# A two-layer hybrid trunk on one core: wider opening products, an earlier filter chain, and a new order of the first opening

## The chip, the cores and the metric

The kernel runs on one core of one Trainium2 chip. The metric is the device time in microseconds (us) of one execution, as the median of several runs. All weights are read from HBM in each run, all arithmetic is float32 or a sum of products whose operands were split into two halves of lower precision.

## The reference, cut to what matters

The input x is 256 rows of 1024 channels. Two layers follow, each a feed-forward block, a mixer of two branches, and a second feed-forward block:

```python
for l in range(DEPTH):                                   # 2
    x = x + 0.5 * swiglu(rms_norm(x), gate, up, down)    # ffn1, d_ff = 2688
    h = rms_norm(x)
    x = x + hybrid_mixer(h, ...)
    x = x + 0.5 * swiglu(rms_norm(x), gate, up, down)    # ffn2

def swiglu(h, w_gate, w_up, w_down):
    return (silu(h @ w_gate) * (h @ w_up)) @ w_down

def hyena_filters(L, w1, b1, w2, b2, w3):                # once a layer, needs no x
    hid = sin(z @ w1 + b1)                               # z: 256 x 33, w1: 33 x 64
    hid = sin(hid @ w2 + b2)                             # w2: 64 x 64
    k = (hid @ w3) * decay                               # w3: 64 x 2048
    full = two_sided(k) * rsqrt(sum(full * full) + EPS)  # unit norm per channel
    return rfft(full)                                    # the spectra of two filters
```

The mixer projects h, runs a Hyena branch (short convolution, two long convolutions by the spectra above) and an attention branch with 12 heads (q and k normed, scores, exp, values), gates the two and projects back.

## The kernel before

All weights pass through one stream of 380 tiles of 128 x 1024 in the order of the list `srcs`: in each layer 65 for ffn1 (among them two for the filters, `fw3`), 62 for the mixer, 63 for ffn2. A tile is loaded into `raw` (four buffers, queue of SP). ACT copies it to `whi` in the short format (line 151), DVE subtracts to get the rest `wlo` (line 58, the line of the helper that records all vector work), both with seven buffers. The activations have the same two halves, `hT[..., 0, :]` (xh) and `hT[..., 1, :]` (xl). A product is three matmuls: wh·xh, wh·xl and wl·xh. One tile feeds 24 matmuls of 256 columns, or 12 of 512.

The stages of an ffn: the **opening** (`opening`, four tiles) makes the first 256 gate and 256 up columns with the tokens as the stationary side, first for token block j = 0 with all four tiles, then for j = 1, since j = 1 is normed later. `xstat` writes the matmuls of one tile and one j. Before the change a tile holds four k-slices of 256 columns of the gate (tiles 0 and 1) or the up weights (tiles 2 and 3). Then 19 pairs of tiles make the remaining columns with the weights stationary, and 21 tiles of the down projection follow. In the very first opening the input has to be squared, normed and transposed first; `warm` products of a zero tile (WARM = 12) run on TensorE before that. `features` transposes the normed x (`xn`) into a PSUM bank, ACT writes the high half of hT and, at a later call, DVE the low half.

Engines run what their queue holds in program order, and the program text is made by a planner. `slot` writes one tile's matmuls, then `passed(UNIT)` takes 2.43 us off `owed`, the vector work that was written and is counted as not yet done (each counted vector instruction adds to it). Before each slot `tick(room)` lets the side chains (`side`) write their next steps while `owed` is under `room` (1.5 us in an ffn, 0.9 to 2.5 in the mixer); a chain that has asked for a wait gets a due time from `owed`, at most 4.86 us. In an opening no slot of j = 0 takes anything off, so `owed` is high when it ends.

Beside ffn1 the side chain `filters` runs: loads into `fc`; a product on 33 rows (`s<-fc`); a sine (eight vector instructions on `sd`, then Sin on ACT, which needs a table load, as does the next Tanh); a product on 64 rows; a second sine; `st`, the third factor; `fw3_unit`, a tile of the main stream; four products with the decay; their squares and sums (`sq`); transposes and a reduction; `rb`, a broadcast on ACT, and its transposes; the scaled `sd`; their halves `hl`; products with the transform matrix `dft`; and the spectra `spec`. All of this twice, once per filter; FW3 = (10, 20) are the pairs m behind which the two `fw3` tiles stand. In the mixer `hyena` and `attention` are the side chains; step n of `attention` writes turn(n - 1), values(n - 2) and scores(n): scores are four products, a reduction on DVE and exp on ACT, `turn` transposes them and copies back, `values` multiplies by v. After the last gate tile the chains are written to their end without other tiles between.

Of the kernel before, what the change touches and what calls it, by code (L numbers as in the profile page):

```python
# [47 lines left out]
def hybrid_trunk(ctx: ExitStack, tc: tile.TileContext, a: dict, out: bass.AP):  # L48
# [88 lines left out]
    def loads(depth=NRAW):  # L137
        while ptr["dma"] < min(len(srcs), ptr["lo"] + depth):
# [3 lines left out]
            nc.sync.dma_start(raws[v][:, :n], src)  # L142
            ptr["dma"] += 1

    def pump_hi():
# [5 lines left out]
        act(out=pairs[v][0][:, :n], in_=raws[v][:, :n], func=AF.Copy)  # L151
# [135 lines left out]
    def normalize(j, mid=None):  # L287
# [4 lines left out]
        if mid is not None:  # L292
            mid()
# [44 lines left out]
    def xstat(acc, i, n, js=(0, 1), c0=0, late=False):  # L338
        kk = DM // n

        def fn(wh, wl):
            for j in js:
                terms = ((0, wh), (1, wh), (0, wl)) if late else ((0, wh), (0, wl), (1, wh))
                for t, (x_, w_) in enumerate(terms):
                    for k in range(kk):
                        g = i * kk + k
                        mm(acc[j][:, c0:c0 + n], hT[:, g, j, x_, :], w_[:, k * n:(k + 1) * n],
                           t == 0 and g == 0, t == 2 and g == KD - 1)
        return fn

    def opening(acc, evac, n):

        us = [use() for _ in range(4)]
        per = n // P

        def part(i, j):
            g, k = divmod(i, per)
            return xstat({j: acc[j][g]}, k, n, (j,), g * n if acc[j][0] is acc[j][-1] else 0, j == 0 and i > 1)

        for i in range(4):  # L360
# [3 lines left out]
            if i in FEAT1:  # L364
                features(1, i - FEAT1[0])()
            for _ in range(FILL[i]):
# [79 lines left out]
    def ffn(l, w, gain, chains=()):  # L446
        with tc.tile_pool(name=nm("ffn"), bufs=1, reuse_waits="tile") as fp:
# [44 lines left out]
            acc = [[bank("acc")] * 2 for _ in range(2)]  # L492

            def first(j):
                t, g, u = t2[:, j, :], acc[j][0][:, :256], acc[j][1][:, 256:]
# [16 lines left out]
            opening(acc, first, 256)  # L512
# [34 lines left out]
    def filters(l):  # L547
        def gen(fp):
            fc = fp.tile([P, S + 2 * P + 2], F32, name=nm("fc"))
            nc.sync.dma_start(fc[:33, :S], a["zT"])  # L550
            nc.sync.dma_start(fc[:33, S:S + P], a["fw1"][l])
            nc.sync.dma_start(fc[:64, S + P:S + 2 * P], a["fw2"][l])
# [30 lines left out]
            mm(b[:, :S], fc[:33, S:S + P], fc[:33, :S], True, True)  # L583
# [3 lines left out]
            mm(b[:, :S], fc[:64, S + P:S + 2 * P], h1[:64, :], True, True)  # L587
# [8 lines left out]
            for o in range(2):  # L596
# [128 lines left out]
    def mixer(l, gain):  # L725
        with tc.tile_pool(name=nm("mix"), bufs=1, reuse_waits="tile") as mp:
# [265 lines left out]
            for blk in range(5):  # L992
# [3 lines left out]
                if blk == 0:  # L996
                    opening([[b] for b in acc], qkv_out(blk, n, acc), n)
# [71 lines left out]
    with tc.manual_schedule():  # L1069
        nc.vector.memset(mhalf, -0.5)  # L1070
        act(out=junk, in_=mhalf[:, :1], func=AF.Tanh)
        warm = spec[:, 0, 0, :P]
# [8 lines left out]
        b = bank("x")  # L1081
        for _ in range(WARM):
            mm(b[:, :P], warm, warm, True, True)
        for h in range(2):
# [147 lines left out]
```

## Time and profile before

| | |
|---|---|
| median of 3 runs | 1120.11 us (1118.97 to 1120.43) |
| profiled execution | 1119.33 us, its span 1117.5 us |
| granted clock, mean | 0.999 |
| TensorE busy | 1102.4 us, 99% |
| VectorE busy | 840.2 us, 75% |
| ScalarE busy | 643.3 us, 58% |
| read from HBM | 204 MB, 184 GB/s |

The times inside the trace count from the start of the span. The profiled execution's own time is 1.8 us longer than its span. A busy TensorE is one that has a matmul in flight; matmuls overlap, so the pace is read from the starts of neighbouring rows. In the list of waits a row gives the engine and the tile that it writes, and after the arrow the engine and the tile that it waited for.

### The profile page before, as it was taken

The page shows a single profiled execution, that of the slowest core. Times are in us where ns is not written, and L with a number is a line of the kernel's source. Part 1 is how long each engine was busy: PE and PEld are TensorE (multiplying, and loading weights), DVE is VectorE, ACT ScalarE, POOL GpSimd, SP SyncE. Part 2 cuts the span into 40 slices and gives each one's busy share as a digit, 9 for nine tenths or more (in the row PEclk, how much of TensorE's full clock was granted, in tenths as well). Part 3 has the DMA queues.
Part 4 walks back from the last instruction along what each step waited for, and adds up shares of the span by engine and source line. Part 5 has one row for each costly group of instructions (what it writes and reads, how often), then busy time and mean ns, then how long its engine had stood idle before and what let it go on. Part 6 is the DMA issues. An engine that isn't in the chain of part 4 may idle for free.

```text
span 1117.5 us, 19195 instructions
## 1 busy us (share of the span) xinstructions
PE 1102.4 (99%) x7591; PEld 1029.3 (92%) x7591; DVE 840.2 (75%) x1243; ACT 643.3 (58%) x983; POOL 64.4 (6%) x113
## 2 busy tenths in 40 slices
PE   9999999999999999999999999999999999999998
PEld 8999988998999999998899998889989998999997
DVE  6779896788865877777567789868888667777772
ACT  6566754665655556666456665547565554666651
POOL 5100000011200000000000000001012000000000
PEclk9999999999999999999999999999999999999999
DMA  8756666556433746667746665737465245666671
GB/s 302 234 168 210 201 212 184 170 171 189 150 115 108 234 140 201 195 193 235 252 147 201 192 209 174 244 110 240 156 185 156 86 125 205 200 192 193 189 256 64
DMA packets 58845, 206.35 MB, mean 185 GB/s; under 512 B 7058, under 2 KB 7718, under 8 KB 58756
## 3 DMA queue, kind: packets, MB, share of 16 engines
q1 hardware_dynamic: 57764, 203.10, 57.3%
q0 software_dynamic: 704, 1.97, 0.6%
q8 instruction: 59, 0.97, 0.4%
q14 instruction: 30, 0.25, 0.1%
q10 hardware_dynamic: 288, 0.07, 0.0%
HBM read 204.00 MB, written 1.11 MB: 184 GB/s over the span
## 4 chain that ended last, share of the span: by engine, by line
PE 82%; DVE 8%; DMA 5%; ACT 3%; issue 2%; POOL 0%; SPq 0%; ACTq 0%; DVEq 0%; POOLq 0%
PE acc L89 54%; PE x L89 13%; PE s L89 12%; DMA raw<-in_gu 4%; DVE wlo L58 3%; PE x L102 2%; DVE spec L58 1%; ACT whi L151 1%; DVE t L58 1%; DVE xn L58 1%; ACT sq L285 1%; DVE x L58 1%; DVE hT L58 1%; PE x L750 1%; PE s L102 0%
## 5 line engine op out<-in xcount | busy, mean ns | idle before, releaser
L58 DVE TENSOR_TENSOR wlo<-raw,whi 128x1024 fp32r<-128x1024 f32 (+1 forms) x380 | 457.6, 1210 | 54.8 <-ACT whi L151 54.5
L151 ACT ACTIVATE whi<-raw 128x1024 fp32r<-128x1024 f32 (+1 forms) x380 | 392.8, 1046 | 142.3 <-PE acc L89 52.6
L89 PE MATMUL acc<-hT,whi 128*128 128x256 f32 (+1 forms) x2416 | 463.5, 290 | 0.0
L89 PEld LDWEIGHTS acc<-hT,whi 128*128 128x128 f32 x2416 | 379.6, 192 | 8.2 <-issue 1.3
L89 PE MATMUL acc<-hT,wlo 128*128 128x256 f32 x1360 | 367.1, 275 | 0.0
L89 PEld LDWEIGHTS acc<-hT,wlo 128*128 128x128 f32 x1360 | 260.9, 192 | 1.9
L89 PE MATMUL acc<-whi,hid 128*128 128x512 f32 (+1 forms) x378 | 115.5, 357 | 0.0
L89 PE MATMUL acc<-whi,hT 128*128 128x256 f32 (+1 forms) x576 | 115.2, 328 | 0.0
L89 PE MATMUL x<-whi,hid 128*128 128x512 f32 x336 | 112.1, 380 | 0.0
L89 PE MATMUL s<-hT,whi 128*128 128x512 f32 x304 | 104.0, 383 | 0.0
L89 PEld LDWEIGHTS acc<-whi,hT 128*128 128x128 f32 x576 | 88.0, 191 | 8.6 <-ACT hT L317 1.1
L89 PEld LDWEIGHTS acc<-whi,hid 128*128 128x128 f32 x378 | 71.0, 189 | 8.6
L89 PE MATMUL s<-hT,wlo 128*128 128x256 f32 x304 | 76.7, 273 | 0.0
L89 PEld LDWEIGHTS x<-whi,hid 128*128 128x128 f32 x336 | 63.6, 189 | 7.9
L89 PE MATMUL acc<-wlo,hid 128*128 128x512 f32 (+1 forms) x189 | 66.4, 356 | 0.0
L89 PEld LDWEIGHTS s<-hT,whi 128*128 128x128 f32 x304 | 57.7, 190 | 6.9 <-DVE c L58 0.7
L89 PE MATMUL acc<-wlo,hT 128*128 128x256 f32 (+1 forms) x288 | 63.4, 324 | 0.4 <-DVE wlo L58 0.2
L89 PE MATMUL x<-wlo,hid 128*128 128x512 f32 x168 | 63.7, 379 | 0.0
L481 ACT ACTIVATE hid<-t 128x256 fp32r<-128x256 f32 x38 | 19.9, 523 | 70.1 <-DVE t L58 70.1
L89 PEld LDWEIGHTS s<-hT,wlo 128*128 128x128 f32 x304 | 58.1, 191 | 1.9
L58 DVE TENSOR_TENSOR hid<-t,hid 128x256 fp32r<-128x256 f32 x76 | 35.5, 466 | 22.4 <-ACT hid L481 22.4
L58 DVE SCALAR_TENSOR_TENSOR t<-t,acc 128x256 f32<-128x256 f32 x46 | 19.2, 417 | 43.0 <-ACT t L457 33.1
(189 smaller groups left out, 1297.4 us busy)
## 6 DMA issues: line engine op xcount, KB each, us to landing
raw<-in_gu SPq DMA_DIRECT2D x152, 512.0 KB, 4.3
raw<-in_dn SPq DMA_DIRECT2D x84, 512.0 KB, 4.4
raw<-in_win_q SPq DMA_DIRECT2D x32, 512.0 KB, 4.0
raw<-in_wg SPq DMA_DIRECT2D x32, 512.0 KB, 4.2
raw<-in_win_h SPq DMA_DIRECT2D x24, 512.0 KB, 4.5
raw<-in_gx SPq DMA_DIRECT2D x16, 512.0 KB, 5.0
raw<-in_wo SPq DMA_DIRECT2D x16, 512.0 KB, 4.1
raw<-in_wp SPq DMA_DIRECT2D x16, 384.0 KB, 3.0
```

Of the source, the lines that this page charges most:

```text
L58: return f(**kw)
L89: nc.tensor.matmul(o, l, r, start=start, stop=stop)
L102: nc.tensor.transpose(b[:, q * P:(q + 1) * P], ap, ident)
L151: act(out=pairs[v][0][:, :n], in_=raws[v][:, :n], func=AF.Copy)
L285: act(out=sq, in_=x[:, j, sl], func=AF.Square, scale=1.0 / 32.0, accum_out=nst[j][:, h:h + 1])
L481: act(out=hi, in_=tv, func=AF.Copy)
L750: nc.tensor.transpose(tb[j][:, (q0 + i) * P:(q0 + i + 1) * P], c[:, i, 1 + j:1 + S:2], ident)
```

## The change

The change has five parts.

The ffn openings use 512-column products: the host lays a tile out as two k-slices of 256 gate and 256 up columns, gate and up of one j share one PSUM bank, and 48 products of 512 columns take the place of 96 of 256. For j = 0 the low halves of the weights now come last in every tile (wh·xh, wh·xl, wl·xh); before, that held for tiles 2 and 3 alone. The mixer's openings, which had 512 columns, get that order too.

In the first opening, `idle` puts a zero product ahead of each term of the first three tiles, nine in all; WARM goes from 12 to 15; tile 0 is loaded in two halves and cast by DVE in two instructions in place of ACT; the calls of the low halves (`los`) and of the pumps stand in another order.

The filter products use all 128 rows: the host pads z, w1 and w2 with zeros, and `fc` is loaded in full (256 KB in place of 83).

At an opening's end `owed` is cut to at most OPEN = 2.0. The filter weights stand sooner: FW3 = (8, 20).

An addition of the skip weights is done for the first of two spectral parts alone (i == 0).

```diff
-WARM = 12
+WARM = 15
+OPEN = 2.0
-FW3 = (10, 20)
+FW3 = (8, 20)
...
-            nc.sync.dma_start(raws[v][:, :n], src)
+            for h in range(2 if v == 0 else 1):
+                sl = slice(h * 512, (h + 1) * 512) if v == 0 else slice(0, n)
+                nc.sync.dma_start(raws[v][:, sl], src[:, sl])
...
-        act(out=pairs[v][0][:, :n], in_=raws[v][:, :n], func=AF.Copy)
+        if by_vector:
+            for h in range(2):
+                sl = slice(h * 512, (h + 1) * 512)
+                dve.tensor_copy(out=pairs[v][0][:, sl], in_=raws[v][:, sl])
+        else:
+            act(out=pairs[v][0][:, :n], in_=raws[v][:, :n], func=AF.Copy)
...
                 for t, (x_, w_) in enumerate(terms):
+                    for _ in range(idle["n"]):
+                        mm(idle["b"], idle["w"], idle["w"], True, True)
...
-            return xstat({j: acc[j][g]}, k, n, (j,), g * n if acc[j][0] is acc[j][-1] else 0, j == 0 and i > 1)
+            return xstat(acc, i, 512, (j,), late=j == 0)
...
+        owed[0] = min(owed[0], OPEN)
...
-            nc.sync.dma_start(fc[:33, :S], a["zT"])
-            nc.sync.dma_start(fc[:33, S:S + P], a["fw1"][l])
-            nc.sync.dma_start(fc[:64, S + P:S + 2 * P], a["fw2"][l])
+            nc.sync.dma_start(fc[:, :S], a["zT"])
+            nc.sync.dma_start(fc[:, S:S + P], a["fw1"][l])
+            nc.sync.dma_start(fc[:, S + P:S + 2 * P], a["fw2"][l])
...
-            mm(b[:, :S], fc[:33, S:S + P], fc[:33, :S], True, True)
+            mm(b[:, :S], fc[:, S:S + P], fc[:, :S], True, True)
...
-            mm(b[:, :S], fc[:64, S + P:S + 2 * P], h1[:64, :], True, True)
+            mm(b[:, :S], fc[:, S + P:S + 2 * P], h1, True, True)
...
-                        if j == 0:
+                        if j == 0 and i == 0:
                             TT(out=t[0:1, :], in0=t[0:1, :], in1=sk[:, o, :], op=ALU.add)
...
-        normalize(0, pump_hi)
+        normalize(0)
+        pump_hi(by_vector=True)
         los = [features(0, 0)]
-        pump(1)
+        pump_hi()
+        los[0]()
+        pump_lo()
         los.append(features(0, 1))
-        los[0]()
-        pump(1)
+        pump_hi()
+        pump_lo()
+        los[1]()
         for h in range(2):
             squares(1, h)
-        los[1]()
         pump_lo()
```

What the change does to the order of instructions is shown at three places. First VectorE in the first opening. A row is one instruction (or several alike), what it writes, and behind the arrow what it reads. Before:

```order
L58 TENSOR_SCALAR v_118<-ss_113 128x1
L58 TENSOR_SCALAR xn_125<-x,r_120 128x512 x2
L58 TENSOR_TENSOR wlo_123<-raw_91,whi_122 128x1024
L58 SCALAR_TENSOR_TENSOR hT<-x_128,gT,hT 128x128 x4
L58 TENSOR_TENSOR wlo_138<-raw_93,whi_137 128x1024
L58 SCALAR_TENSOR_TENSOR hT<-x_143,gT,hT 128x128 x4
L58 TENSOR_TENSOR wlo_157<-raw_95,whi_156 128x1024
L58 TENSOR_SCALAR v_174<-ss_162 128x1
```

And after:

```order
L59 TENSOR_SCALAR v_122<-ss_117 128x1
L59 TENSOR_SCALAR xn_126<-x,r_124 128x512 x2
L157 CAST whi_129<-raw_91 128x512 x2
L59 SCALAR_TENSOR_TENSOR hT<-x_133,gT,hT 128x128 x4
L59 TENSOR_TENSOR wlo_130<-raw_91,whi_129 128x1024
L59 TENSOR_TENSOR wlo_143<-raw_94,whi_142 128x1024
L59 SCALAR_TENSOR_TENSOR hT<-x_152,gT,hT 128x128 x4
L59 TENSOR_TENSOR wlo_162<-raw_96,whi_161 128x1024
L59 TENSOR_SCALAR v_179<-ss_171 128x1
```

The two casts of tile 0 are new, the first low half of the features moved ahead of the first `wlo`, and the second behind that of tile 1.

Second VectorE around `st` in ffn1 of layer 0. `t` and `hid` belong to the evacuation of a pair of tiles. Before, with the `wlo` of tiles 22, 23 and 24:

```order
L58 TENSOR_TENSOR wlo_891<-raw_784,whi_890 128x1024
L58 SCALAR_TENSOR_TENSOR t_964<-t_964,acc_883 128x256
L58 TENSOR_TENSOR t_964<-t_964,acc_883 128x256
L58 TENSOR_TENSOR wlo_931<-raw_824,whi_930 128x1024
L58 TENSOR_TENSOR hid_217<-t_964,hid_198 128x256
L58 TENSOR_TENSOR st_997<-sd_240,st_997 64x256
L58 TENSOR_TENSOR dft_76<-bias,dft_75 128x512
L58 TENSOR_TENSOR wlo_962<-raw_857,whi_961 128x1024
```

And after, with those of tiles 16, 17 and 18:

```order
L59 TENSOR_TENSOR wlo_660<-raw_548,whi_659 128x1024
L59 SCALAR_TENSOR_TENSOR t_729<-t_729,acc_648 128x256
L59 TENSOR_TENSOR t_729<-t_729,acc_648 128x256
L59 TENSOR_TENSOR wlo_696<-raw_591,whi_695 128x1024
L59 TENSOR_TENSOR hid_219<-t_729,hid_200 128x256
L59 TENSOR_TENSOR st_762<-sd_245,st_762 64x256
L59 TENSOR_TENSOR dft_76<-bias,dft_75 128x512
L59 TENSOR_TENSOR wlo_727<-raw_622,whi_726 128x1024
```

`st` moved from behind tile 23 to behind tile 17. TensorE reads it with the `fw3` tile, which is tile 22 (whi_890) before and tile 18 (whi_726) after.

Third TensorE at the end of the mixer of layer 0, from the last gate tile's last product to the first product of the merge (`u`). Before:

```order
L89 MATMUL acc_4092<-hT,wlo_3840 128x256
L102 MATMUL x_4200<-ident,at_3593 128x128 x4
L89 MATMUL x_4206<-v_2432,at_3593 128x64 x4
L89 MATMUL x_4213<-v_2432,at_3593 128x64 x4
L956 MATMUL x_4220<-ident,ya_4040 128x128 x2
L89 MATMUL acc_4229<-u_2422,whi_3878 128x256
```

And after:

```order
L90 MATMUL acc_4028<-hT,wlo_3782 128x256
L103 MATMUL x_4142<-ident,at_3593 128x128 x4
L90 MATMUL x_4148<-v_2396,odd_3586 128x64 x4
L90 MATMUL x_4155<-qkT_3240,odd_3585 128x128
L90 MATMUL x_4155<-qkT_3435,odd_3585 128x128
L90 MATMUL x_4155<-qkT_3435,odd_3586 128x128
L90 MATMUL x_4155<-qkT_3240,odd_3585 128x128
L103 MATMUL x_4164<-ident,at_3593 128x128 x4
L90 MATMUL x_4170<-v_2396,at_3593 128x64 x4
L90 MATMUL x_4177<-v_2396,at_3593 128x64 x4
L967 MATMUL x_4184<-ident,ya_4081 128x128 x2
L90 MATMUL acc_4193<-u_2386,whi_3820 128x256
```

turn(6), values(5) and scores(7) (the products with qkT) moved from ahead of the last gate tile to behind it. The same holds in layer 1.

## Rows read from the trace of the kernel before

**Rows 1.** The page's part 1: busy us, share of the span, instructions.

```profile
PE 1102.4 (99%) x7591; PEld 1029.3 (92%) x7591; DVE 840.2 (75%) x1243; ACT 643.3 (58%) x983; POOL 64.4 (6%) x113
```

**Rows 2.** TensorE's waits, 40 to 145 us: us in total, times, longest.

```profile
PE s L102 <- DVE sq L58: 1.5, 1, 1.5
PE x L89 <- DVE st L58: 1.2, 1, 1.2
PE s L102 <- ACT rb L642: 1.0, 1, 1.0
PE s L89 <- DVE hl L58: 0.9, 1, 0.9
PE s L89 <- ACT sd L578: 0.6, 1, 0.6
...
```

**Rows 3.** TensorE's waits, 570 to 700 us (ffn1 of layer 1).

```profile
PE s L89 <- DVE hl L58: 1.4, 1, 1.4
...
```

**Rows 4.** Timeline, TensorE around sq: start, us, engine, operation, [idle before <- releaser].

```profile
103.37 0.28 PE L89 MATMUL acc<-hT,wlo 128*128 128x256 f32 x1
...
105.12 0.66 PE L102 MATMUL s<-ident,sq 128*128 128x128 f32 x4 [1.48 <-DVE sq L58]
```

**Rows 5.** Timeline of the first opening.

```profile
1.08 5.49 PE L89 MATMUL x<-spec 128*128 128x128 f32 x24 [1.08 <-DVE spec L1073]
...
7.47 1.14 ACT L311 ACTIVATE hT<-x,gT 128x128 fp32r<-128x128 f32 x4
...
8.70 1.12 DVE L58 SCALAR_TENSOR_TENSOR hT<-x,gT,hT 128x128 fp32r<-128x128 f32 x4
...
9.74 1.22 DVE L58 TENSOR_TENSOR wlo<-raw,whi 128x1024 fp32r<-128x1024 f32 x1
10.87 1.12 DVE L58 SCALAR_TENSOR_TENSOR hT<-x,gT,hT 128x128 fp32r<-128x128 f32 x4
...
13.91 0.88 DVE L58 TENSOR_SCALAR xn<-x,r 128x512 f32<-128x512 f32 x2 [0.67 <-POOL r L291]
...
22.57 0.39 PE L89 MATMUL acc<-hT,whi 128*128 128x256 f32 x2
```

**Rows 6.** Timeline, TensorE: products of 256 columns, then of 512 columns.

```profile
17.86 1.06 PE L89 MATMUL acc<-whi,hT 128*128 128x256 f32 x8
...
18.76 0.61 PE L89 MATMUL acc<-wlo,hT 128*128 128x256 f32 x4
...
206.40 1.03 PE L89 MATMUL acc<-whi,hT 128*128 128x512 f32 x4
207.26 0.59 PE L89 MATMUL acc<-wlo,hT 128*128 128x512 f32 x2
```

**Rows 7.** Timeline, TensorE: the filter product on 33 rows and what follows.

```profile
44.54 0.70 PE L89 MATMUL s<-fc 33*128 33x256 f32 x2
45.16 0.38 PE L89 MATMUL acc<-hT,whi 128*128 128x256 f32 x1
```

**Rows 8.** Windows: length, busy us of PE, PEld, DVE, ACT, POOL, then clock, DMA, GB/s.

```profile
20.00:30.00 10.00, 10.00 (x92) 10.00 (x91) 5.40 (x7) 5.33 (x7) 9.81 (x47) 1.00 0.93 314
...
75.00:105.00 30.00, 28.64 (x248) 28.24 (x248) 27.49 (x42) 19.09 (x29) 0.00 (x0) 1.00 0.68 210
```

**Rows 9.** Timeline, VectorE after the first sine.

```profile
59.35 0.42 DVE L58 SCALAR_TENSOR_TENSOR t<-t,acc 128x256 f32<-128x256 f32 x1 [3.12 <-ACT t L457]
```

**Rows 10.** Timeline at the end of the mixer of layer 0.

```profile
352.21 0.47 PE L89 MATMUL acc<-hT,whi 128*128 128x256 f32 x2
...
353.86 0.19 ACT L934 ACTIVATION_READ_ACCUMULATOR at<-at,mx 128x1 f32 x1
...
357.17 1.10 PE L89 MATMUL x<-v,at 128*128 128x64 f32 x8 [0.76 <-ACT at L939]
```

**Rows 11.** Timeline: wlo of tiles 9 and 10, and tile 10's first product.

```profile
30.49 2.35 DVE L58 TENSOR_TENSOR wlo<-raw,whi 128x1024 fp32r<-128x1024 f32 x2
...
39.08 0.39 PE L89 MATMUL acc<-hT,whi 128*128 128x256 f32 x2
```

More of the change, by code (lines that the diff above doesn't have):

```diff
@@ L291, in normalize @@
         pool.tensor_tensor(out=r, in0=v, in1=mhalf[:, :1], op=ALU.pow)
-        if mid is not None:
-            mid()
         xn = gbp.tile([P, DM], F32, tag="xn", name=nm("xn"))
@@ L336, in wstat_wide, with xstat @@
         return fn
-    def xstat(acc, i, n, js=(0, 1), c0=0, late=False):
+    def xstat(acc, i, n, js=(0, 1), late=False):
         kk = DM // n
@@ L344, in fn, with opening @@
                 for t, (x_, w_) in enumerate(terms):
+                    for _ in range(idle["n"]):
+                        mm(idle["b"], idle["w"], idle["w"], True, True)
                     for k in range(kk):
                         g = i * kk + k
-                        mm(acc[j][:, c0:c0 + n], hT[:, g, j, x_, :], w_[:, k * n:(k + 1) * n],
+                        mm(acc[j][:, :n], hT[:, g, j, x_, :], w_[:, k * n:(k + 1) * n],
                            t == 0 and g == 0, t == 2 and g == KD - 1)
         return fn
-    def opening(acc, evac, n):
+    idle = {"n": 0}
+    def opening(acc, evac):
         us = [use() for _ in range(4)]
-        per = n // P
         def part(i, j):
-            g, k = divmod(i, per)
-            return xstat({j: acc[j][g]}, k, n, (j,), g * n if acc[j][0] is acc[j][-1] else 0, j == 0 and i > 1)
+            return xstat(acc, i, 512, (j,), late=j == 0)
         for i in range(4):
@@ L365, in opening @@
                 features(1, i - FEAT1[0])()
+            if i == 2:
+                idle["n"] = 0
             for _ in range(FILL[i]):
@@ L490, in ffn @@
             sls = (slice(0, S), slice(S, 2 * S))
-            acc = [[bank("acc")] * 2 for _ in range(2)]
+            acc = [bank("acc") for _ in range(2)]
             def first(j):
-                t, g, u = t2[:, j, :], acc[j][0][:, :256], acc[j][1][:, 256:]
+                t, g, u = t2[:, j, :], acc[j][:, :256], acc[j][:, 256:]
                 act(out=t, in_=g, func=AF.Tanh, scale=0.5)
@@ L510, in turn @@
                 yield True
-            opening(acc, first, 256)
+            opening(acc, first)
             side.extend(gens)
@@ L996, in mixer @@
                 if blk == 0:
-                    opening([[b] for b in acc], qkv_out(blk, n, acc), n)
+                    opening(acc, qkv_out(blk, n, acc))
                     gens = [hyena(), attention()]
@@ L1071, in hybrid_trunk @@
         act(out=junk, in_=mhalf[:, :1], func=AF.Tanh)
-        warm = spec[:, 0, 0, :P]
+        warm = spec[:, 0, 3, :P]
         nc.vector.memset(warm, 0.0)
@@ L1159, in _constants @@
     order = np.concatenate([np.arange(0, L, 2), np.arange(1, L, 2)])
-    zT = z[order].T
+    zT = np.zeros((P, L), f)
+    zT[:z.shape[1]] = z[order].T
     lo = math.log(1e-2) / 1.5
@@ L1185, in _layout @@
         g = [A[f"ffn{w}_w_{n}"] for n in ("gate", "up")]
-        first = [_laced(t[:, :, :256], 256).reshape(L, 2, 4, P, 256).transpose(0, 1, 3, 2, 4).reshape(L, 2, P, 1024) for t in g]
-        o[f"gx{w}"] = np.concatenate(first, 1)
+        first = _laced(np.concatenate([t[:, :, :256] for t in g], 2), 512)
+        o[f"gx{w}"] = first.reshape(L, 4, 2, P, 512).transpose(0, 1, 3, 2, 4).reshape(L, 4, P, 1024)
         rest = [t[:, :, 256:].reshape(L, KD, P, MF - 2, P).transpose(0, 3, 2, 1, 4) for t in g]
@@ L1207, in _layout @@
     o["skip"] = A["hy_skip"]
-    o["fw1"] = np.concatenate([A["hy_filt_w1"]] * 2, 2)
-    o["fw2"] = np.concatenate([A["hy_filt_w2"]] * 2, 2)
+    for n, t in (("fw1", A["hy_filt_w1"]), ("fw2", A["hy_filt_w2"])):
+        o[n] = np.zeros((L, P, P), t.dtype)
+        o[n][:, :t.shape[1]] = np.concatenate([t] * 2, 2)
     o["fw3"] = _laced(np.concatenate([A["hy_filt_w3"]] * 2, 1), 512)
```

7 lines of the change are left out of this document (4 added, 3 removed).

## The prediction, made before the changed kernel was run

> **What bounds the kernel now.** I read the busy shares first: TensorE 99 per cent of the span, VectorE (DVE) 75, ScalarE (ACT) 58 [rows 1]. So time can only come from two places: the pace of the matmuls, and the places where TensorE stands still. Then I read TensorE's waits, stretch by stretch. Between 40 and 145 us, the first feed-forward stage of layer 0, six waits stand, 5.4 us in sum: a square sum from DVE (sq) 1.5, the third filter factor (st) 1.2, a broadcast by ACT (rb) 1.0, a low half (hl) 0.9, a sine (sd) 0.6 [rows 2], and a spectrum 0.2, whose row is left out. All belong to the filter chain that runs beside the gate and up products. The same stage of layer 1 has hl 1.4 [rows 3], and rb and a spectrum of 0.2 each, rows left out: 1.8 us. Each wait costs more than its row, since the next matmul also fills the array anew: around the sq wait the starts lie 105.12 - 103.37 = 1.75 us apart, and 0.11 is the pace, so 1.64 is lost for a wait of 1.48 [rows 4]. With some 0.2 each the six are 5.4 + 1.2 = 6.6 us, the three of layer 1 about 2.2.
>
> The profiled execution took 1119.33 us, its span 1117.5; the sums below are made against 1119.33. The median of the runs is 0.78 higher, and I add that at the end.
>
> **1. The first opening: +1.2 us.** Three more warm products are 6 records. The 24 of now take 5.49, 0.23 each [rows 5]; six cost 1.4 at that pace and 0.7 at the 0.1125 a record of the later products [rows 6]. xn, for which the transposes wait now, gives a little room: I take 0.8, with bounds 0 and 1.4. ACT's first feature group, now 7.47 to 8.61, waits for the transposes and then ends at about 9.2 [rows 5]. DVE casts tile 0 meanwhile, which hides in its idle time (two pieces of 512 columns; bounded from both sides by the row of two such xn pieces, 0.88, and by the subtract of 1024 columns, 1.22). But its next instruction is now the low half of the features, not wlo of tile 0, and it waits for ACT. Behind it on DVE stand in this order: low half A (1.04), wlo 0 and 1 (1.14 each), low half B (1.04), wlo 2 (1.14), v, 0.7 for the power on GpSimd, xn of the second row block. From 9.26: 10.3, 11.4, 12.6, 13.6, 14.8, 15.0, and xn at 15.65, where it stands at 13.91 now [rows 5]. Everything after it follows: wlo 3 at about 16.5 to 17.7, tile 3's last products to 18.1, the second transposes to 18.55, then 24 products of 512 columns, 5.2. The opening ends at about 23.75, against 22.57: +1.2. The nine zero products (two such records, 0.22 each) lie in waits for DVE and cost nothing; without that cover they are 2.0. If the transposes were not pushed, low half A would start at 8.6, where ACT ends now, and the end be +0.6. Range +0.3 to +1.8.
>
> **2. The other openings: -0.7 us.** 8 products of 256 columns take 18.76 - 17.86 = 0.90, 0.1125 each; 4 of 512 columns 207.26 - 206.40 = 0.86, 0.215 each [rows 6]. An opening's second half, 48 of the first against 24 of the second, so falls from 5.40 to 5.16: -0.24 in each of three. In its first half TensorE is ahead of wlo of tile 3 and what it saves it waits, so I count nothing there (bounds -0.24 and 0 each). The mixer's openings had 512 columns already; only the order of their terms changes: 0.
>
> **3. Full-row filter products: -0.8 us.** The 33-row product of two records takes 45.16 - 44.54 = 0.62, 0.31 a record [rows 7], that of 64 rows as much; there are 8 records in the two layers. No full-row one of this kind is in the trace. A record's work is at most that of one 512-column product, 0.215 [rows 6]; at that pace 8 x 0.095 = 0.8 is saved. Bounds 0 and -1.6 (0.1125 a record).
> The Trainium skill, "TensorE: Matmul & The Clock Gate", section "Why this matters for your kernels", states against this that a single matmul on 32 rows takes the time of one on 128. By it this term would be 0 and the sum 0.8 higher. The row with 33 rows shows a slower record than the 512-column rows do, but not why.
> The larger loads, 256 KB in place of 83, are 0.55 us of the DMA at 314 GB/s [rows 8]; they delay the weight tiles behind them on SP's queue by that. wlo of tile 10 ends at 32.84 and is first used at 39.08, 6.2 us later [rows 11], and that lead hides it; without that cover it is 0.55 a layer.
>
> **4. The filter chain of layer 0: -4.1 us.** Owed vector work is cut to 2.0 at an opening's end, so the planner starts the chain at once: the first filter product stands behind tile 4 where it stood behind tile 11, the second behind 9 (15), fw3's behind 18 (22), the square sum's transposes behind 28 (32), rb's behind 30 (34), the hl products behind 36 and 40 (41 and 42). What counts is how far DVE or ACT must be ahead of TensorE for each. st stands behind wlo 17 for a product behind tile 18, where it stood behind wlo 23 for one behind 22: from one tile ahead to one behind, so this wait goes. sd now needs two tiles of lead in place of three, rb four in place of five, the second hl three in place of five, the last spectrum two in place of four. A tile is 2.7 us, more than any of these waits, so I let them go: 0.8 + 1.4 + 1.2 + 1.1 + 0.3 = 4.8. sq needs three tiles before and after. Its 1.7 stays, and grows a little: four tiles sooner DVE has 4 x 1.14 = 4.6 us of wlo and two evacuations less to do, and TensorE is 10.7 sooner; what pays the rest is idle time of DVE that the chain can fill (busy 5.40 of 10 us in 20 to 30) [rows 8], though not the 3.12 behind the sine on ACT [rows 9]. I take 0.7 for that. -4.8 + 0.7 = -4.1. Bounds -6.6 (all go) and -1.5.
>
> **5. The chain of layer 1: -1.5 us.** The waits are 1.8 us in sum [rows 3], 2.2 with the refills. The positions move as in layer 0 (second hl from five tiles ahead to three), sq had no wait and may get one. Two thirds: -1.5; bounds -2.2 and 0.
>
> **6. The mixers' ends: +2.2 us.** The attention starts one tile later. Behind the last gate tile now stand turn(7), values(6), values(7), outs; after the change turn(6), values(5), scores(7) and then these. scores(7) is a chain with nothing beside it: products, a reduce on DVE, exp on ACT, transposes. Now a gate tile covers it: the products end at 352.21, ACT ends at 353.86 + 0.19 = 354.05 [rows 10]. Bare, TensorE waits 1.85. In return the copy that values(7) waits for, now behind the last gate's tanh on ACT (0.76) [rows 10], comes free earlier: 1.85 - 0.76 = 1.1 a layer. Bounds 0 and +3.7. Four additions of one partition less on DVE, and the mixer's middle: 0.
>
> **Sum.** 1119.33 + 1.2 - 0.7 - 0.8 - 4.1 - 1.5 + 2.2 = 1115.6; with 0.78, **1116.4 us** by the median.
>
> **Rivals.**
> *A, the waits move.* DVE is the next bound: 27.49 of 30 us busy between 75 and 105 [rows 8]. Each chain step comes sooner, but so does its due time, and DVE has the same work in less time; sq's wait grows to what st and rb give back. Terms 4 and 5 are then -1.5 and -0.7: 1119.0, by the median 1119.8. For it: sq's position; against it: the lead needed falls for five of the six.
> *B, slower.* The sines now start where wlo is ahead by only 39.08 - 32.84 = 6.2 us [rows 11]. Each sine leaves DVE idle for some 3.1 behind ACT's table load and sine [rows 9]: the two use up 2 x 3.1 = 6.2, all of that lead, and their own vector work, at least the half of such a stretch, comes on top. TensorE waits 1.5 for wlo in tiles 10 to 18, and with DVE late from there on sq, rb and hl come no sooner for TensorE than now. It decides from a lead under 7.7 at the first sine, if nothing is won back between the two. Terms 4 and 5 are 0 and 1.5 is added: 1122.7, by the median 1123.5. Against it: idle time of DVE before the sines [rows 8], which lets the lead grow first.
> *C, all goes.* DVE's idle 4.6 us in 20 to 30 and more up to 60 take the chain whole; all nine waits go: -6.6 and -2.2, 1112.4, by the median 1113.2. Against it: sq needs as much lead as before.
> *D, rows don't matter.* The record with 33 rows is slow for another reason than its rows (a small first operand, a switch of type), and the full-row one is as slow: term 3 is 0, 1117.2 by the median.
> The page of the Trainium skill that part 3 names states that rule.
>
> **Chances.** Forecast 0.43, A 0.24, C 0.13, D 0.10, B 0.10. The range runs from C's lower side to A's, 1112.5 to 1120.0, and leaves out B and half of C's spread. A measurement can tell about 0.2 per cent here, 2.24 us: faster is under 1117.9. The forecast and D are mostly there, C is: faster 0.61; A and the rest: same 0.29; slower 0.10.
>
> **What would show it.** In the trace after: tile 4's first product at 23.5 to 24 us (term 1), xn's second pair at 15 to 16; records of the filter products 0.2 apart (term 3); between 35 and 140 us one long wait, for sq, and none for st, rb, sd (term 4); behind the last gate tile a TensorE wait for exp on ACT of 1.5 to 2 us (term 6). Wrong if TensorE waits for wlo between tiles 8 and 20 (B), if sq's wait is over 3 us (A), or if the opening's end is not later than now.

## The result: slower by one per cent

The changed kernel takes 1132.38 us (median of 4 runs, 1130.0 to 1133.25), the kernel before 1120.27 beside it: a ratio of 1.0107, 95% interval 1.0089 to 1.0124, or 12 us. I had forecast 1116.4 and a range of 1112.5 to 1120.0. The profiled execution takes 1130.0, its span 1128.2, 10.7 more than that of before.

The stages, from the first weight product of each to the first of the next (the first of all from the span's start), show where the 10.7 us lie (us, from the starts on TensorE's timeline):

| stage | before | after | difference |
|---|---|---|---|
| ffn1, layer 0 | 199.0 | 198.4 | -0.6 |
| mixer, layer 0 | 198.1 | 203.3 | +5.2 |
| ffn2, layer 0 | 167.9 | 167.7 | -0.2 |
| ffn1, layer 1 | 184.1 | 185.3 | +1.2 |
| mixer, layer 1 | 198.1 | 203.5 | +5.4 |
| ffn2, layer 1, to its last product | 167.0 | 166.9 | -0.1 |

The loss is in the two mixers. I had given them +2.2 together, and some -5.4 to the two ffn1 (the filter chains and products, and their openings), which lose 0.6.

### The profile page after: what moved, and what is told of

Read it like the earlier page. It is cut to its first block, busy times and chain, and to the rows that moved or that the text cites. A ratio compares the mean times of both kernels' runs of the same rounds, so it can differ in the third digit from the quotient of the medians.

```text
span 1128.2 us, 18872 instructions
## 1 busy us (share of the span) xinstructions
PE 1106.0 (98%) x7423; PEld 1029.3 (91%) x7423; DVE 839.4 (74%) x1241; ACT 641.7 (57%) x982; POOL 63.2 (6%) x113
## 4 chain that ended last, share of the span: by engine, by line
PE 82%; DVE 7%; ACT 4%; DMA 4%; issue 1%; POOL 1%; ACTq 0%; DVEq 0%; SPq 0%
PE acc L90 54%; PE x L90 13%; PE s L90 13%; DMA raw<-in_gu 3%; DVE wlo L59 3%; PE x L103 2%; ACT whi L159 2%; DVE t L59 1%; DMA raw<-in_win_h 1%; DVE sd L59 1%; DVE spec L59 1%; POOL rs L888 1%; ACT L468 0%; PE s L103 0%; PE x L761 0%
## 5 line engine op out<-in xcount | busy, mean ns | idle before, releaser
L90 PE MATMUL acc<-hT,whi 128*128 128x256 f32 (+1 forms) x2416 | 470.1, 292 | 5.6 <-DVE t L59 5.6
L90 PEld LDWEIGHTS acc<-hT,whi 128*128 128x128 f32 x2416 | 385.1, 194 | 13.4 <-issue 5.9
L90 PEld LDWEIGHTS acc<-hT,wlo 128*128 128x128 f32 x1360 | 263.6, 194 | 2.0
L90 PE MATMUL acc<-whi,hT 128*128 128x512 f32 (+1 forms) x448 | 114.4, 371 | 0.3 <-DVE hT L59 0.2
L90 PEld LDWEIGHTS acc<-whi,hT 128*128 128x128 f32 x448 | 78.2, 190 | 12.2 <-DVE hT L59 2.5
L90 PE MATMUL acc<-wlo,hT 128*128 128x512 f32 (+1 forms) x224 | 62.9, 368 | 1.0 <-DVE wlo L59 0.9
```

Of the source, the lines that this page charges most:

```text
L90: nc.tensor.matmul(o, l, r, start=start, stop=stop)
```

## The profile after

The busy time of the engines hardly changed; this is the page's part 1, to be read against [rows 1]:

```profile
PE 1106.0 (98%) x7423; PEld 1029.3 (91%) x7423; DVE 839.4 (74%) x1241; ACT 641.7 (57%) x982; POOL 63.2 (6%) x113
```

TensorE's waits over the whole span (us in total, times, longest) answer to [rows 2, 3]:

```profile
PE acc L90 <- DVE t L59: 5.6, 2, 3.5
PE x L103 <- DVE qk L59: 4.5, 2, 2.3
PE x L103 <- ACT at L945: 3.3, 2, 1.6
PE s L103 <- DVE sq L59: 1.5, 1, 1.5
...
PE s L103 <- ACT rb L653: 0.4, 1, 0.4
```

The waits for st, hl and sd are gone, as forecast. The wait for sq, which the forecast kept in ffn1 of layer 0, is gone there, and its 1.5 us now stand in layer 1. Three pairs stand above it, one wait of each in each layer: for `t`, the evacuation of a pair in ffn1 (3.5 and 2.1); for `qk`, in the mixer; and for `at`, behind the mixer's last gate tile, 1.6 in place of the 0.76 of [rows 10]. The first two are new.

**The wait for t.** The timeline of ffn1 in layer 0 (start, us, engine, operation, what ended the idle time):

```profile
46.98 1.28 ACT L589 ACT_TABLE_LOAD   x1
...
50.57 0.29 DVE L59 TENSOR_SCALAR sd<-sd 128x256 f32<-128x256 f32 x1
50.90 0.42 ACT L589 ACTIVATE sd<-sd 128x256 f32<-128x256 f32 x1 [2.64 <-DVE sd L59]
51.23 1.04 ACT L159 ACTIVATE whi<-raw 128x1024 fp32r<-128x1024 f32 x1
52.28 1.28 ACT L468 ACT_TABLE_LOAD   x1
53.58 0.38 ACT L468 ACTIVATE t<-acc 128x256 f32<-128x256 f32 x1
...
55.01 0.77 PE L90 MATMUL acc<-hT,whi 128*128 128x256 f32 x2 [3.45 <-DVE t L59]
```

ACT loads the table for the second Sin at 46.98 and then stands still until DVE has finished the argument at 50.9. The Tanh of an evacuation is behind it in ACT's queue, and it needs the other table back. So `t` comes at 53.58, the bank `acc` comes free late, and TensorE, which had its next weights long since, waits 3.45 us.

**The wait for qk.** The same view in the mixer of layer 0, after, and then two rows of before:

```profile
222.08 3.82 POOL L888 TENSOR_TENSOR rs<-ss,mhalf 128x16 f32<-128x16 f32 x1 [20.64 <-DVE ss L59]
...
225.93 0.69 DVE L59 TENSOR_TENSOR qk<-qk,rs 128x512 f32<-128x512 f32 x1 [2.80 <-POOL rs L888]
...
226.77 0.63 PE L103 MATMUL x<-ident,qk 128*128 128x128 f32 x4 [2.27 <-DVE qk L59]
```

```profile
228.40 3.84 POOL L877 TENSOR_TENSOR rs<-ss,mhalf 128x16 f32<-128x16 f32 x1 [26.33 <-DVE ss L58]
...
240.31 0.60 PE L102 MATMUL x<-ident,qk 128*128 128x128 f32 x4
```

The power of the norm takes GpSimd 3.8 us in both kernels. Before, the transposes came 8 us after its end. Now they stand five tiles sooner in TensorE's queue (the second set six), and it waits for GpSimd and DVE.

**The clock.** In or just behind the waits for t (layer 0) and qk (both layers) the granted clock is halved, from 2.4 to 1.2 GHz. Windows (length, busy us of PE, PEld, DVE, ACT, POOL, then clock) around the waits for t and for qk:

```profile
51.00:54.00 3.00, 0.56 (x6) 0.37 (x4) 0.01 (x1) 2.93 (x4) 0.00 (x0) 0.94 0.18 67
54.00:57.00 3.00, 1.99 (x9) 2.02 (x10) 2.96 (x5) 2.10 (x3) 0.00 (x0) 0.50 0.00 0
57.00:60.00 3.00, 3.00 (x16) 3.00 (x15) 2.87 (x6) 1.99 (x6) 0.00 (x0) 0.50 0.88 232
60.00:63.00 3.00, 3.00 (x27) 3.00 (x26) 2.77 (x4) 2.15 (x3) 0.00 (x0) 0.92 0.73 265
...
224.00:227.00 3.00, 0.73 (x7) 0.57 (x6) 1.07 (x2) 1.08 (x3) 1.90 (x1) 1.00 0.59 175
227.00:230.00 3.00, 3.00 (x20) 3.00 (x19) 3.00 (x7) 1.63 (x2) 0.00 (x0) 0.62 0.34 97
```

Between 57 and 60 us TensorE starts 16 products, where it starts 27 in a window at nearly full clock. Where neighbouring starts lie at about twice their distance at full clock, the excess sums to 2.4 us behind the wait for t and 1.5 behind each wait for qk: 5.4 us in this execution, beside the waits. The trace of before has no such stretch. All four executions have some: their mean granted clock is 0.992 to 0.997, against 0.999 for the profiled execution of before. At half the pace half of a stretch is lost, so what a run can lose by it is at most the missing share of its span: 3.4 to 9 us here.

**The first opening.** It ends at 23.25, and its second xn stands at 15.03:

```profile
1.08 5.88 PE L90 MATMUL s<-spec 128*128 128x128 f32 x30 [1.08 <-DVE spec L1084]
6.80 1.09 PE L103 MATMUL x<-ident,xn 128*128 128x128 f32 x8
...
15.03 0.88 DVE L59 TENSOR_SCALAR xn<-x,r 128x512 f32<-128x512 f32 x2 [0.67 <-POOL r L299]
...
23.25 0.38 PE L90 MATMUL acc<-hT,whi 128*128 128x256 f32 x2
```

## The experiments

Ratios are to the kernel before on the same chip, with their 95% interval; 0.1 per cent is 1.1 us. The mean granted clock of a run, where it is given, is that of the whole span.

### First, which part loses: the cut, and where

The theory from the traces: the cut of `owed` at the end of the mixer openings is the loss. The rivals: the wider openings and the first opening, or the ffn cut itself.

**The cut in ffn openings only** (changed kernel):

```diff
-        owed[0] = min(owed[0], OPEN)          # in opening()
...
             opening(acc, first)               # in ffn()
+            owed[0] = min(owed[0], OPEN)
```

> The changed kernel, with the cut of owed vector work only at the end of ffn openings; the mixers' steps then stand where they stood before. Theory 1 (the loss is the cut in the mixers: transposes of qk too soon, and the scores behind the last gate tile): the two mixers give back 5.2 and 5.4 us, so about 1121.5 against 1132.4, level with the kernel before within 2 us; no wait for qk and none of 1.8 for exp. Theory 2 (the mixers lose through the other edits, the new order of their opening's terms or the clock): they stay 5 us slower, 1130 to 1132. The long wait of ffn1 for the evacuation t (3.5 us, and 5 us at the lower clock) stays in both.

Measured: 1.0019 (1.0001 to 1.0037), 1121.63 us. The waits for qk are gone, those for at are back at 0.8 each, and those for t stand (5.5 in sum). The mixers' loss went with the cut there: in the profiled execution they are 1.8 and 0.3 us longer than before, and the 1.8 has a stretch at the lower clock behind a wait of 0.8 for at.

**The cut in mixer openings only** (kernel before):

```diff
                     opening([[b] for b in acc], qkv_out(blk, n, acc), n)
+                    owed[0] = min(owed[0], 2.0)
```

> The kernel before, with the cut in the two mixer openings as the only edit. Theory 1: all of the mixers' loss appears alone, +10 us, about 1130.5, with the waits for qk (2.3 each) and for exp (1.6 each) in both layers. Theory 2: under +2 us. My forecast priced this at +2.2, the scores alone.

Measured: 1.0092 (1.0059 to 1.0125), 1127.79, five runs from 1124.3 to 1133.31. Its waits:

```profile
PE x L103 <- DVE qk L59: 4.5, 2, 2.3
PE x L103 <- ACT at L935: 3.3, 2, 1.6
```

They are those of the changed kernel to the tenth. This one line is most of the loss. The profiled execution is the fastest of the five and has no stretch at the lower clock; its mixers are 4.0 us longer each, and the other runs up to 9 us more in all. Two of the five, 1124.3 and 1127.79, have a mean granted clock of 1.000, so the new order costs 6 us or more without any help of the clock; the two slowest, 1132.53 and 1133.31, have 0.994 and 0.992.

**No cut, filter weights at 10 and 20** (changed kernel):

```diff
-FW3 = (8, 20)
+FW3 = (10, 20)
...
-        owed[0] = min(owed[0], OPEN)
```

> The changed kernel without the cut, the filter weights where they stood (10 and 20): first opening, 512-column products and full-row filter products alone. By the trace of after: opening +0.7, filter products -0.8, other openings -0.2 each: about -0.7, so 1119.6, the same within the noise; the filter waits of before (5.4 and 1.8) come back. Were the wider openings or the first opening the loss, it would be over 1122.

Measured: 1.0023 (1.0008 to 1.0037): slower, where I had expected -0.7 us. The wait for sd is 2.6, where it was 0.6; why it grew was not tested.

**The cut in ffn openings and the earlier filter weights only** (kernel before):

```diff
-FW3 = (10, 20)
+FW3 = (8, 20)
...
             opening(acc, first, 256)
+            owed[0] = min(owed[0], 2.0)
```

> The kernel before, with the cut in the ffn openings and the earlier filter weights only. By the two traces the first stage of layer 0 gains 6.5 of waits and loses 3.5 for t and some 2.6 at the lower clock; layer 1 loses 1.2. So 1119 to 1122, no gain. My forecast of the same edit was -4.1 - 1.5 = -5.6, 1114.7. If the low clock and the wait for t are absent here, the other edits caused them and my forecast stands.

Measured: 0.9992 (0.9978 to 1.0007), no difference. This is the edit for which I had forecast -5.6. Its two main waits:

```profile
PE s L103 <- DVE sq L59: 3.5, 2, 2.3
PE acc L90 <- DVE t L59: 1.8, 1, 1.8
```

The waits of [rows 2, 3] moved to sq, in both layers now, and to t. The three parts add up: +0.92 of the mixer cut, +0.23 without any cut, -0.08 of the ffn cut are +1.07 per cent, what the whole change costs. That they meet to the last digit is luck, since each has an interval of 0.15 to 0.33 either way.

### Second, the mechanisms of the two waits, and the other parts alone

**Sin held one step** (on the version with the cut in ffn openings only):

```diff
+                yield True
                 act(out=dst, in_=arg, func=AF.Sin)
```

> The kernel with the cut in ffn openings only, and one step of waiting put ahead of each Sin on ACT, so that ACT's queue holds the Sin only when its argument is counted as done on DVE. Theory 3 (TensorE's waits of 3.0 and 2.5 for t come from ACT: Sin stands ahead of the Tanh that frees the bank of acc, and Sin itself waits for DVE's sine arithmetic): both waits fall under 1 us, no stretch at the lower clock in ffn1, 3 to 6 us faster than without it, about 1116 against 1118.3 of before. Theory 4 (DVE has too much work in these tiles, wherever Sin stands): the waits stay within 1 us of 3.0 and 2.5, or come back as waits for wlo, and the time stays at +0.2 per cent.

Measured: 1.0010 (0.9997 to 1.0022). The waits for t are gone, which is theory 3. The time hardly follows:

```profile
PE s L103 <- DVE sq L59: 4.3, 2, 2.3
PE s L90 <- ACT sd L590: 1.9, 2, 1.7
```

What t no longer costs, sq and sd do. The place of Sin makes the wait for t. That the work on DVE in these tiles makes that there is some wait is my reading, not tested apart.

**Half of the power** (changed kernel; half of the norm of q and k is left out):

```diff
-                pool.tensor_tensor(out=rs.rearrange("p j h -> p (j h)"), in0=ss.rearrange("p j h -> p (j h)"),
-                                   in1=mhalf, op=ALU.pow)
+                pool.tensor_tensor(out=rs[:, 0, :], in0=ss[:, 0, :], in1=mhalf[:, :8], op=ALU.pow)
...
-                       in1=rs[:, j, :].rearrange("p (h o) -> p h o", o=1)
+                       in1=rs[:, 0, :].rearrange("p (h o) -> p h o", o=1)
```

> The changed kernel in its own order, but GpSimd takes the power for 8 of its 16 columns in the norm of q and k, and both token blocks are scaled by these 8 (the other half of that norm is left out). Theory 5 (the new waits for qk are the 3.8 us of GpSimd, which the planner does not count): with half of its time the waits of 2.3 us fall by 1.9 each, and the stretches at the lower clock behind them go; 4 to 8 us less than the changed kernel, 1122.5 to 1126.5 on a chip where before takes 1118.3. If the wait is for DVE's own backlog, it stays at 2.3 and the time at +1 per cent.

Measured: 1.0103 (1.0077 to 1.0129). GpSimd and the wait:

```profile
225.46 2.56 POOL L888 TENSOR_TENSOR rs<-ss,mhalf 128x8 f32<-128x8 f32 x1 [21.32 <-DVE ss L59]
...
PE x L103 <- DVE qk L59: 2.0, 2, 1.0
```

GpSimd is 1.26 us shorter (not 1.9, so half the columns are two thirds of the time) and the waits fall from 4.5 to 2.0 in sum, 1.25 each. That is theory 5 for the wait. The stretches at the lower clock behind qk are gone from this trace, and its first mixer is 3.2 us longer than before in place of 5.2. The time, for which I had expected 4 to 8 us less, did not fall by more than the runs scatter: this profiled execution has 2.6 us of lower clock behind the wait for at in layer 1, which the changed kernel's has not, and the mean granted clock of the four runs is 0.989 to 0.997. So the wait is settled by this run, and its price in time is not.

**Full-row filter products only** (kernel before):

```diff
-            nc.sync.dma_start(fc[:33, :S], a["zT"])
+            nc.sync.dma_start(fc[:, :S], a["zT"])
...
-            mm(b[:, :S], fc[:33, S:S + P], fc[:33, :S], True, True)
+            mm(b[:, :S], fc[:, S:S + P], fc[:, :S], True, True)
...
-            mm(b[:, :S], fc[:64, S + P:S + 2 * P], h1[:64, :], True, True)
+            mm(b[:, :S], fc[:, S + P:S + 2 * P], h1, True, True)
```

> The kernel before, with the full-row filter products and their full loads alone. My term: -0.8. The records should stand 0.22 apart in place of 0.31. If the larger loads delay the weight stream where ACT waits for it (1.3 to 2.1 us between 22 and 50 us), the wait for sd grows from 0.6 to 2 or more and the edit costs 1 us or more.

Measured: 1.0017 (1.0002 to 1.0031), slower or the same, not faster. On TensorE the records behave as in the changed kernel (its rows are shown below), and the wait for sd is 0.8, not 2. Its profiled execution has three stretches at the lower clock, one in the first opening, which this edit does not touch. I can't tell the loads from such accidents here.

**Openings only** (kernel before with the 512-column openings, their order of terms, and the fewer skip additions):

```diff
-            return xstat({j: acc[j][g]}, k, n, (j,), g * n if acc[j][0] is acc[j][-1] else 0, j == 0 and i > 1)
+            return xstat(acc, i, 512, (j,), late=j == 0)
...
-                        if j == 0:
+                        if j == 0 and i == 0:
```

> The kernel before, with 512-column products and the new order of terms in all openings, and the fewer skip additions, alone; first opening's other edits, filter products and planner as before. My term: -0.7 for three openings and some more for the first, and 0 in the mixers; by the trace of after -0.2 in each ffn opening and 0 to +0.3 in the mixers'. So -1.0 to 0. If the filter waits move by more than 1 us here too, the time of the chain is sensitive to a shift of half a microsecond, whatever the edit.

Measured: 0.9987 (0.9973 to 1.0002), 1116.64 against 1118.93. Seven of ten runs lie between 1115.65 and 1116.74, three between 1119.9 and 1120.65. Those three have a mean granted clock of 0.997 or 0.998, the seven have 0.998 to 1.000, five of them 1.000.

### Third, the first opening, the late attention, and the clock

**Openings with the changed first opening** (on the version with the openings alone):

```diff
-WARM = 12
+WARM = 15
...
+        idle.update(n=1, b=b[:, :P], w=warm)
...
-        normalize(0, pump_hi)
+        normalize(0)
+        pump_hi(by_vector=True)
         los = [features(0, 0)]
-        pump(1)
+        pump_hi()
+        los[0]()
+        pump_lo()
```

> The 512-column openings with the changed first opening (15 warm products, zero products, tile 0 in two loads and cast by DVE, the new order), without the full-row filter products and without any cut. Against the openings alone (-2.3) it shows the first opening: by the trace of after +0.65 at the opening's end, so -1.6; my term was +1.2, so -1.1. If the later start of the weight stream is what feeds the longer filter waits of the version with all three, 0 to +1.

Measured: 1.0010 (0.9997 to 1.0023), against 0.9987 without them (the intervals just overlap): by the ratios the first opening costs 2.5 us, though its end is only 0.6 later (23.15 against 22.54). In the profiled execution st waits 2.1 in sum and hl 1.9; the openings alone have 1.8 and none for hl. So the chain seems to pay again, though no step of it was moved against that version.

**Attention one step late** (kernel before):

```diff
+                yield True
+                yield True
                 for n in range(11):
```

> The kernel before, with the attention started one step later and nothing else: behind the last gate tile stand turn(6), values(5) and scores(7) as in the changed kernel. My term 6: +1.1 a layer, +2.2. By the trace of after the wait for exp is 1.6 in place of 0.8 a layer, so +1.6, and 1.2 to 1.5 more in each execution in which the clock falls behind that wait. If the mixers' loss lay here and not in the qk transposes, +8 or more.

Measured: 1.0057 (1.0036 to 1.0078). In layer 1 of the profiled execution the mixer takes 1.0 us more than before, which is my term 6 nearly to the tenth. In layer 0 it is 3.9, and the windows show why:

```profile
356.00:360.00 4.00, 2.94 (x15) 2.94 (x15) 0.51 (x5) 1.41 (x3) 0.00 (x0) 0.65 0.27 107
360.00:364.00 4.00, 3.83 (x19) 3.54 (x19) 1.66 (x5) 0.38 (x1) 0.00 (x0) 0.50 0.00 0
```

The clock falls behind the wait for exp, and the slower pace costs 2.7 us in this stretch.

**The same with seven products in the wait:**

```diff
                 def turn(n):
                     b = bank("x")
+                    for _ in range(7 if n == 7 else 0):
+                        mm(b[:, :P], ident, ident, True, True)
```

> The kernel with the attention one step late (+5.6 to +6.4 alone), and seven products of the identity matrix, 1.5 us, ahead of the transposes of turn(7), which lie in the wait of 1.6 us for exp. Theory 6 (of these 6 us only some 2 are the longer chain, and the rest is the lower clock behind the wait): the clock stays at 1.00 behind it and the median falls to +1 to +3. If the chain itself costs the 6 us, the median stays.

Measured: 1.0020 (1.0008 to 1.0033). The intervals of the two do not overlap. Seven products that compute nothing, in a place where TensorE waited, take some 4 us off. Seven of the ten runs have a mean granted clock of 1.000; the four without the filling have 0.992 to 0.995. What is left, +0.20 per cent, is 2.2 us, and in the profiled execution each mixer is 1.0 us longer than before. The windows answer to those above:

```profile
356.00:360.00 4.00, 3.92 (x35) 3.69 (x34) 1.13 (x5) 1.41 (x3) 0.00 (x0) 1.00 0.45 151
360.00:364.00 4.00, 3.74 (x34) 3.55 (x34) 1.57 (x3) 1.23 (x2) 0.00 (x0) 1.00 0.15 16
```

**Ten products ahead of the qk transposes** (kernel before with the mixer cut):

```diff
                     b = bank("x")
+                    for _ in range(10 if blk == 0 and j == 0 else 0):
+                        mm(b[:, :P], ident, ident, True, True)
                     transpose4(b, [qk[:, j, q * P:(q + 1) * P] for q in range(4)])
```

> The kernel before with the cut in the mixer openings (+10.3 alone), and ten products of the identity matrix with itself, 2.2 us, ahead of the first transposes of qk in each layer, which lie in the wait of 2.3 us. Theory 6 (a part of the loss is the clock that falls after a wait, 1.2 to 1.6 us each time): the clock stays at 1.00 behind the qk wait and the median falls by 1 to 3 us, to +7 to +9. If only the wait itself counts, the median stays at +10, or rises by what the products push.

Measured: 1.0072 (1.0048 to 1.0096), against 1.0092 without them. The direction is the expected one; the intervals overlap. The trace stays at 1.00 throughout, and its mixers are 3.9 us longer each, as without the filling and without a stretch.

**Both fillings in the changed kernel**, the two diffs above:

> The changed kernel with both fillings, ten products ahead of the first transposes of qk and seven ahead of turn(7), in both layers. Theory 6: the stretches at the lower clock in the mixers go, and of +12 some 3 to 6 go with them, so +6 to +9; the wait for t in ffn1 with its own stretch stays. If the clock is a side matter, +11 to +13.

Measured: 1.0067 (1.0050 to 1.0084) against 1.0107, without overlap (1.0084 and 1.0089). So by the medians 4 of the 12 us are the clock behind the mixers' two waits. In the profiled execution the mixers have no stretch at the lower clock and are 3.8 and 4.1 us longer than before, in place of 5.2 and 5.4. The four runs lie within 0.8 us of each other.

**Parts that gained or cost nothing, together** (on the openings alone):

```diff
-FW3 = (10, 20)
+FW3 = (9, 20)
...
             opening(acc, first)
+            owed[0] = min(owed[0], 2.0)
...
+                yield True
                 act(out=dst, in_=arg, func=AF.Sin)
```

> The parts that gained or cost nothing, put together: 512-column openings with their order of terms and the fewer skip additions, the cut in ffn openings only, Sin held one step, filter weights at 9 and 20; the first opening and the filter products as before. By the single runs: -2.3 for the openings, -0.3 to -1 for the cut, -1 for the held Sin, and the square sum two tiles later than with 8: 1114 to 1116 where before takes 1118.5. If the filter's waits only change places, it stays at the openings' -2.3, 1116.5 or above.

Measured: 0.9983 (0.9964 to 1.0002), 1116.89. Not better than the openings alone; a wait for sd of 3.3 took the place of those for sq and t, with a stretch at the lower clock behind it.

**Openings with fillings ahead of waits of before** (on the openings alone; the zero products of the first opening, and):

```diff
                 def values(n):
...
+                    for _ in range(3 if n == 7 else 0):
+                        mm(b[:, :P], ident, ident, True, True)
...
+                for _ in range(4 if o == 0 else 0):
+                    mm(b[:, :P], ident, ident, True, True)
                 transpose4(b, [sq[:, c * P:(c + 1) * P] for c in range(4)])
```

> The 512-column openings alone (-2.3), with filling products ahead of three of the waits that the kernel had before: zero products in the first opening, three products ahead of values(7), four ahead of the first transposes of the square sum. Theory 6: fewer executions with a stretch at the lower clock, so less scatter and a median of -2.5 to -4 (1115 to 1116.5). If the scatter has other causes, as the openings alone, with the same scatter (1115.6 to 1120.7); if the products push the chain, -1 to 0.

Measured: 0.9988 (0.9978 to 0.9999), 1118.28 against 1119.03. The scatter is smaller, 1116.39 to 1119.0, and all eleven runs have a mean granted clock of 1.000, but the median is not below that of the openings alone: the fillings hold the clock and bring no time here. Of all versions this is the only one whose interval lies below 1, by a hair.

## Why the prediction was wrong

**Term 6, the mixers (forecast +2.2, measured +10.6).** The part that I worked out, scores(7) behind the last gate tile, was right: +1.0 in the undisturbed layer. The step that failed is the last half sentence of that part, "and the mixer's middle: 0". In the new order the transposes of qk stand five to six tiles sooner, and the prediction does not ask what they wait for. GpSimd's 3.8 us stood in the trace of before, covered by 8 us. By the program's text the planner counts vector work alone and gives the step a due time from `owed`; with `owed` cut to 2.0 this is shorter than GpSimd's power. The halved power shows the wait follow GpSimd one to one. Without a stretch at the lower clock a mixer is 3.8 to 4.1 us longer (the cut in mixer openings, with and without its filling, and both fillings): 1.0 for the scores, 2.4 between the starts around the wait for qk, and the rest in small waits.

**The clock (not in the prediction).** I priced each wait by its row and 0.2 us of refill [rows 4]. Behind the new waits of 1.6 us and more the clock can fall to 1.2 GHz, and that costs some 1.5 to 2.7 us again. The trace of before showed none of it. In the mixers that is about 4 of the 12 us, by the fillings.

**Terms 4 and 5, the filter chain (forecast -5.6, measured about -0.9 with an interval from -2.5 to +0.8).** The waits that I let go did go, and others came. The step that failed is "a tile is 2.7 us, more than any of these waits, so I let them go". It counts positions in a queue as if the queues ran on as before. I named the right rival, A, and its mechanism: with these two edits alone sq grew to 3.5 in sum. In the whole changed kernel it did not, there the wait for t took its place. I named neither the wait for t nor its cause. B had the sines as the place of a new wait, but through wlo; it came through a PSUM bank that ACT freed late.

**Term 3 (forecast -0.8, measured -1.6 on TensorE).** The direction was right, the size was half. The rows of before around [rows 7], then those of after:

```profile
44.33 0.28 PE L89 MATMUL acc<-hT,wlo 128*128 128x256 f32 x1
...
45.49 0.28 PE L89 MATMUL acc<-hT,wlo 128*128 128x256 f32 x1
```

```profile
25.82 0.28 PE L90 MATMUL acc<-hT,wlo 128*128 128x256 f32 x1
25.93 0.60 PE L90 MATMUL s<-fc 128*128 128x256 f32 x2
26.18 0.57 PE L90 MATMUL acc<-hT,whi 128*128 128x256 f32 x2
26.59 0.28 PE L90 MATMUL acc<-hT,wlo 128*128 128x256 f32 x1
```

From one of these wlo rows to the next lie the same five records, two of the filter and three others: 45.49 - 44.33 = 1.16 before and 26.59 - 25.82 = 0.77 after. Less three of 0.11 that is 0.82 for a filter product before and 0.43 after, -0.39 for each of four. The forecast's 0.62 is read from the first filter record to the next product; it leaves out that the record ahead and the one behind took longer too (0.21 to the next start, where 0.11 is the pace). So the sentence of the Trainium skill ("TensorE: Matmul & The Clock Gate", "Why this matters for your kernels"), that a single matmul on 32 rows takes the time of one on 128, does not hold for these float32 products on 33 and 64 rows where they stand, and rival D is out. In the time the gain does not show, and where it goes is not shown.

**Term 1 (forecast +1.2, measured +0.7 at the opening's end).** Mis-sized: the six records push the transposes from 6.64 to 6.80, not by 0.8, as the 30 take 5.88 in place of 5.49. The row of before:

```profile
6.64 1.23 PE L102 MATMUL x<-ident,xn 128*128 128x128 f32 x8
```

DVE's chain of low halves was as I had it, and xn comes 1.1 later, not 1.7. Half a microsecond at the start may cost two more in the chain, if the pair of versions with and without it is taken at its ratios; their intervals just overlap, so this is not shown.

**Term 2 (forecast -0.7).** -0.2 in each of three, right for the trace. Openings alone gain 2.3 by the medians, 1.5 by the ratio, with an interval that just reaches 0. One addition fewer in each filter is in that; the first opening's end hardly moved (22.54 against 22.57). In its profiled execution 2.2 us of the gain are in ffn1 of layer 0, behind the opening, where the chain fell better.

## What to carry to other kernels

When a planner's constant is loosened, every step that it places moves, and the price is not in the steps that one wanted to move. Go through the moved steps that end in a matmul, and ask of each which engine comes last ahead of it, and whether the planner counts that engine; a wait that is covered by 8 us shows in no list of waits. A function that needs another table on ACT is better queued when its argument is ready, since all evacuations stand behind it; here that took the wait for t away, but no time with it that the runs can tell.

## What the runs showed of the hardware that I had not expected

A wait of TensorE can cost more than its length. Behind waits of 1.6 to 3.5 us the granted clock was 0.5 for some 3 to 7 us, in some executions and not in others (behind qk in the changed kernel, not with the mixer cut alone), at some 1.5 to 2.7 us each. Products with no use in the wait kept it at 1.00 and gave back about 4 us in two comparisons; in a third the difference, 2 us, is within the intervals. Shorter waits can do it as well: five versions whose mixers end as the kernel before does (the cut in ffn openings on either kernel, the full rows, the openings with the first opening, and the parts put together) show one such stretch each near a mixer's end, where the longest wait is 0.8 us.

A part of the scatter of the kernel before goes with these stretches. Of its 95 runs on the four chips of the experiments, the 43 with a mean granted clock of 1.000 lie 0.6 us below their chip's median on average, the 41 with 0.998 lie 0.6 above it, and the 8 with 0.997 or 0.996 lie 2.0 above it; the other three have 0.999. It is a part alone: the runs at 1.000 still spread by up to 3.5 us to either side. What else scatters, and what decides whether the clock falls behind a given wait, stays open.
